# Attention probabilities transposed in 32x32 blocks on VectorE with a transfer through DRAM, and decay matrices with the step size in the exponent

## The chip, the cores and the metric

One Trainium2 chip, one core. The metric is the device time of one execution of the whole kernel in microseconds (us), the median of several timed runs. A profile of one further execution shows every instruction of the engines: PE (TensorE: matmuls, and transposes as matmuls with an identity), PEld (its weight loads), DVE (VectorE), ACT (ScalarE), POOL (GpSimd) and SP, whose queue issues the transfers (DMAs).

## The reference

One layer of a bidirectional encoder over 512 tokens of width 1024, in float32. One projection feeds a state-space branch (Mamba-2 SSD, both directions, 32 heads in 8 groups, chunks of 128 tokens) and a windowed attention branch (16 query heads on 4 key/value heads, width 64, blocks of 128 queries that see 3 blocks of keys, and 2 at either end). Gates merge the branches, an output projection and an MLP follow. The two parts that the change touches, cut to what matters:

```python
# attention, per head and block of 128 queries; keys are 2 or 3 blocks of 128
logits = where(valid, q @ k.T * 64 ** -0.5 + bias, -inf)
m = maximum(logits.max(-1), sink)
p = exp(logits - m)
p = p / (p.sum(-1) + exp(sink - m))
out = p @ v

# SSD within a chunk, per head and direction; cs = cumsum(dt * a)
decay = where(tril, exp(cs[l] - cs[s]), 0)
y_diag[l] = sum over s of (c[l] . b[s]) * decay[l, s] * dt[s] * x[s]
```

## The kernel before

The program is a list of *quanta*. Most are one 128-row tile of a projection: 8 or 16 steps over the contracted dimension, each with three matmuls of 128x512 (`mm3`), since every float32 operand is split into a high and a low part (ACT casts the high part, POOL or DVE subtracts it for the low one). A weight chunk of 512 KB comes by a transfer that SP issues into one of `RAW` = 3 raw buffers and is split into one of `SPL` = 3 pairs of buffers, ahead of the quantum that uses it (`chunk_raw`, `chunk_split`, `prefetch`).

Beside the quanta run *acts*: functions placed at a position between quanta (`at`, `place_head`, `place_ssd`). A position only sets where an act stands in the recorded program. At the end `Planner` reads the whole program with its dependencies, gives every instruction a cost and a due time, and fixes the order of each engine's queue (`chain`). So each engine runs in a fixed order, an instruction that waits holds up those behind it on its own engine, and a change of any operation can move others.

Attention, per head `h`: `attn_bias` loads a bias tile (L849). `attn_scores` makes the scores of 4 query blocks in PSUM, adds the bias and takes the row maximum (DVE, L865), Exp with a sum (ACT, L874), the sums' reciprocal (DVE), and scales each block of probabilities by it (DVE, L880). `attn_flip` transposes the probabilities on PE (L410, 10 blocks of 128x128 a head) into PSUM and copies them out, half on ACT and half on DVE (L891). `attn_values`, for a pair of heads, multiplies the values with them, the two heads side by side in column halves of the array. `HEADS` places the scores at 0, the flip 2 and the values 3.5 quanta behind a head's position; by `JOIN` the values of two pairs are done at one place, four such places in all.

SSD, per group and chunk `c`: `load` brings the rows cs of both directions from DRAM, the same to all partitions (`rf`, `rb`), `similar` the products C.B of two chunks, multiplied by the two triangular masks (L1114), and `prep` makes from them the matrix `m` for 4 heads: POOL subtracts cs from `rb` (L1123), ACT from `rf` (L1125, four pieces of 128), DVE takes the minimum (L1126), ACT Exp (L1127); ACT multiplies the masked products by the step size dt in both directions (L1129 and L1130, eight pieces), DVE adds them and multiplies by the decay (L1131, L1132). `within` uses `m` on PE.

Tiles of 512 columns come from `Slots`, a ring of 73 numbered places that are given out in the order in which they came free.

Of the kernel before, what the change touches and what calls it, by code (L numbers as in the profile page):

```python
# [26 lines left out]
SLOTS, RAW, SPL, PP, AHEAD, SPARE = 73, 3, 3, 3, 4, 6  # L27
# [14 lines left out]
HEADS = dict(scores=0, flip=2, values=3.5)  # L42
# [20 lines left out]
class Slots:  # L63


    def __init__(self, pool, n, tags):
        self.pool, self.free, self.slot, self.n, self.tags = pool, deque(range(n)), {}, 0, tags

    def get(self, name, shape=(128, 512), dtype=F32):
        s = self.free.popleft()  # L70
        self.n += 1
        t = self.pool.tile(list(shape), dtype, tag=f"s{s}", name=f"{name}_{self.n}", bufs=1)
        self.tags[t.tensor.name] = f"s{s}", 1
        self.slot[id(t)] = (s, t)
        return t

    def put(self, *tiles):
        for t in tiles:
            self.free.append(self.slot.pop(id(t))[0])


class Planner:
# [57 lines left out]
    def region(ap):  # L140
# [3 lines left out]
        if step == 0 or ap.tensor.name.startswith(("brow", "csT", "csE", "rrow")):  # L144
# [120 lines left out]
    def transfer(self, n):  # L265
# [3 lines left out]
        rows = {"rrow": 70, "csT": 120, "csE": 100, "in_w_in": 270, "in_w_mlp_in": 270, "in_w_ssd_out": 270, "in_w_attn_out": 270}  # L269
        return size / rows.get(src.tensor.name.rsplit("_", 1)[0].rstrip("01234567") if src.tensor.name.startswith(("cs", "rrow")) else src.tensor.name, 100 if size < 2 ** 17 else 310)  # L270
# [76 lines left out]
class Trunk:  # L347
    def __init__(self, ctx, tc, ins, out, dbg=None):
# [392 lines left out]
    def dt_math(self):  # L741
# [25 lines left out]
        def sums():  # L767
# [7 lines left out]
            nc.vector.tensor_scalar(self.ncs, self.cs, -1.0, None, op0=ALU.mult)  # L775
# [75 lines left out]
    def attn_scores(self, h):  # L851
# [26 lines left out]
        for n in range(4):  # L878
            p, w = P[n]
            nc.vector.tensor_scalar(p[:, :w], p[:, :w], sm[:, n:n + 1], None, op0=ALU.mult)  # L880
        self.P[h] = P

    def attn_flip(self, h):
        self.T[h] = []
        for n, (p, w) in enumerate(self.P.pop(h)):
            pt = self.bank("ps")
            for b in range(w // 128):
                self.tr(pt[:, b * 128:(b + 1) * 128], p[:, b * 128:(b + 1) * 128])
# [2 lines left out]
            (self.nc.vector.tensor_copy if n % 2 else self.nc.scalar.copy)(pT[:, :w], pt[:, :w])  # L891
# [142 lines left out]
    def ssd_steps(self, g):  # L1034
# [71 lines left out]
        def similar(j):  # L1106

            pc, both = self.bank("ps"), get("cb", (128, 2, 2, 128))
# [5 lines left out]
            nc.vector.tensor_tensor(both, products.to_broadcast([128, 2, 2, 128]),  # L1114
# [707 lines left out]
```

## Time and profile before

| what | value |
|---|---|
| timed runs | 1075.16, 1075.75, 1075.84 us; median 1075.75 |
| span of the profiled execution | 1073.7 us; its time beyond the span is not recorded by itself, the timed median is 2.0 us above it |
| TensorE clock granted | 0.999 of full speed |
| DMA | 152.21 MB, mean 142 GB/s |
| attention | DVE reads scores from 51.7 us, PE transposes 58.6 to 328.8, PE values 124.8 to 342.9 |
| last matmul starts | 1067.4 us |

The span is from the first to the last instruction of one execution. "Busy" is time in which an engine runs something; matmuls overlap, so the distance between their starts, not their duration, is what each one takes from PE. "Idle before" is idle time of the engine just before an instruction, with what ended it. A view by windows gives busy us and instructions (x) of each engine in a stretch.

### The profile page before, as it was taken

Reading aid. Unit: us, or ns where it says so; the run is one execution under the profiler, and the core shown is the slowest. Engines: PE = TensorE matmul, PEld = TensorE weight load, DVE = VectorE, ACT = ScalarE, POOL = GpSimd, SP = SyncE. Lnnn points to the kernel's source line nnn. Section 1 sums busy time; section 2 is a strip of 40 time slices with the busy share of each in tenths; the row PEclk is TensorE's granted clock in tenths of the full one; section 3 lists DMA queues with packets and bytes.
Section 4 is the critical chain, followed back from the end, with each engine's and each line's share of the span. In section 5 each row is a group of like instructions: output and inputs, shape, how many; then the busy total and the mean of one; then the engine's idle time right before and its main releaser. Section 6 shows DMA issues by size and latency. Waiting matters only on the chain.

```text
span 1073.7 us, 16828 instructions
## 1 busy us (share of the span) xinstructions
PE 1065.3 (99%) x5560; PEld 898.7 (84%) x5560; DVE 783.9 (73%) x1330; ACT 656.4 (61%) x1413; POOL 809.5 (75%) x1007
## 2 busy tenths in 40 slices
PE   9999999999999999999999999999999999999997
PEld 7888888888888888888888888889888888888886
DVE  6677886798786877778875868769853754764888
ACT  5568776777676867775876522476755444444444
POOL 4546558567648988999998878665999888888853
PEclk9999999999999999999999999999999999999999
DMA  7536425634545655466645399855713512512422
GB/s 209 152 92 165 125 71 143 147 85 133 147 111 146 174 161 158 127 140 177 180 123 133 106 272 323 259 174 150 222 41 93 177 44 88 174 53 75 142 98 79
DMA packets 221560, 152.21 MB, mean 142 GB/s; under 512 B 12541, under 2 KB 195045, under 8 KB 221472
## 3 DMA queue, kind: packets, MB, share of 16 engines
q1 hardware_dynamic: 221324, 151.06, 49.3%
q8 instruction: 44, 0.72, 0.3%
q14 instruction: 44, 0.36, 0.1%
q10 hardware_dynamic: 148, 0.07, 0.0%
HBM read 138.19 MB, written 12.91 MB: 141 GB/s over the span
## 4 chain that ended last, share of the span: by engine, by line
PE 97%; DVE 1%; DMA 0%; ACT 0%; SPq 0%; issue 0%; DVEq 0%; ACTq 0%
PE pp L406 68%; PE ps L406 26%; PE ps L410 4%; DVE x L1731 0%; DMA wr<-in_w_in 0%; DVE C L954 0%; DVE acc L1692 0%; DVE ag L1726 0%; SPq L578 0%; DVE C L961 0%; ACT junk L1712 0%; ACT C L950 0%; DVE junk L627 0%; ACT th L960 0%; SPq L701 0%
## 5 line engine op out<-in xcount | busy, mean ns | idle before, releaser
L406 PE MATMUL pp<-b,wh 128*128 128x512 f32 (+1 forms) x1840 | 564.6, 387 | 0.0
L485 POOL TENSOR_TENSOR wl<-wr,wh 128x256 fp32r<-128x256 f32 (+1 forms) x503 | 416.2, 858 | 137.6 <-ACT wh L481 127.8
L406 PEld LDWEIGHTS pp<-b,wh 128*128 128x128 f32 x1840 | 341.4, 188 | 68.2 <-issue 0.9
L406 PE MATMUL pp<-b,wl 128*128 128x512 f32 (+1 forms) x920 | 355.5, 387 | 0.0
L406 PEld LDWEIGHTS pp<-b,wl 128*128 128x128 f32 x920 | 172.8, 188 | 34.2
L481 ACT CAST wh<-wr 128x1024 fp32r<-128x1024 f32 x131 | 136.3, 1041 | 87.7 <-PE pp L406 65.0
L1646 POOL TENSOR_TENSOR wl<-wd,wh 128x256 fp32r<-128x256 f32 x168 | 147.6, 909 | 39.5 <-ACT wh L1642 25.1
L1642 ACT CAST wh<-wd 128x512 fp32r<-128x512 f32 x108 | 62.9, 619 | 59.9 <-PE pp L406 32.1
L406 PE MATMUL ps<-wh,fh 128*128 128x512 f32 (+1 forms) x196 | 75.5, 385 | 0.5 <-DVE acc L1692 0.5
L406 PE MATMUL ps<-wl,fh 128*128 128x512 f32 (+1 forms) x196 | 75.4, 385 | 0.0
L406 PE MATMUL ps<-wh,fl 128*128 128x512 f32 (+1 forms) x196 | 75.4, 385 | 0.0
L1520 DVE SCALAR_TENSOR_TENSOR pp<-pp,r 128x512 f32<-128x512 f32 (+1 forms) x31 | 17.6, 567 | 67.9 <-ACT r L1517 67.9
L1129 ACT ACTIVATE n<-cb,tables 128x128 f32<-128x128 f32 x128 | 48.9, 393 | 9.4 <-DVE cb L1114 8.9
L1646 POOL TENSOR_TENSOR wl<-wt,wh 128x256 fp32r<-128x256 f32 x56 | 45.8, 849 | 11.0 <-ACT wh L1642 5.7
L1130 ACT ACTIVATE m<-cb,tables 128x128 f32<-128x128 f32 x128 | 49.2, 393 | 5.0 <-DVE cb L1114 3.1
L954 DVE SCALAR_TENSOR_TENSOR u<-pp,cv,u 128x510 f32<-128x510 f32 (+1 forms) x64 | 47.7, 746 | 4.8 <-ACT u L950 3.3
L874 ACT ACTIVATE P<-P,mx 128x384 f32<-128x384 f32 (+1 forms) x64 | 35.2, 552 | 19.1 <-DVE mx L871 18.9
L1181 POOL TENSOR_TENSOR w<-w,E 128x256 f32<-128x256 f32 x48 | 39.5, 838 | 8.7 <-DVE E L1153 7.9
L1123 POOL TENSOR_TENSOR rb<-rb,tables 128x512 f32<-128x512 f32 x32 | 36.4, 1141 | 10.4 <-DMA rb<-csT 10.4
L1125 ACT ACTIVATE rf<-rf,tables 128x128 f32<-128x128 f32 x128 | 42.0, 392 | 2.6 <-DMA rf<-csT 2.5
L406 PEld LDWEIGHTS ps<-wh,fh 128*128 128x128 f32 x196 | 36.8, 188 | 8.1 <-DVE acc L1692 0.7
L406 PEld LDWEIGHTS ps<-wh,fl 128*128 128x128 f32 x196 | 36.8, 188 | 7.4
(304 smaller groups left out, 2064.5 us busy)
## 6 DMA issues: line engine op xcount, KB each, us to landing
wr<-in_w_in SPq DMA_DIRECT2D x74, 512.0 KB, 4.2
wr<-in_w_mlp_in SPq DMA_DIRECT2D x32, 512.0 KB, 4.3
wd<-in_w_mlp_out SPq DMA_DIRECT2D x64, 256.0 KB, 4.0
rb<-csT SPq DMA_DIRECT2D x32, 256.0 KB, 4.9
rf<-csT SPq DMA_DIRECT2D x32, 256.0 KB, 5.1
wr<-in_w_ssd_out SPq DMA_DIRECT2D x14, 512.0 KB, 5.7
wd<-in_w_o SPq DMA_DIRECT2D x28, 256.0 KB, 5.4
E<-csE SPq DMA_DIRECT2D x96, 64.0 KB, 4.8
```

The costliest lines, as they stand in the source:

```text
L406: self.nc.tensor.matmul(out, lhsT, rhs, start=start, stop=stop, skip_group_check=more)
L410: self.nc.tensor.transpose(out, src, self.ident[:n, :n])
L481: self.nc.scalar.copy(hi[:, :m], raw)
L485: engines[e].tensor_tensor(lo[:, c], raw[:, c], hi[:, c].bitcast(F32), op=ALU.subtract)
L954: nc.vector.scalar_tensor_tensor(u[:, a:e], ps[:, a + d:e + d], self.wtap(t, b), u[:, a:e], op0=ALU.mult, op1=ALU.add)
L1123: nc.gpsimd.tensor_tensor(v4(rb), v4(rb), cs[:, 1].unsqueeze(2).to_broadcast([128, 4, 128]), op=ALU.subtract)
L1125: nc.scalar.activation(v4(rf)[:, h], v4(rf)[:, h], AF.Identity, bias=ncs[:, 0, h:h + 1])
L1129: nc.scalar.activation(v4(n)[:, h], cb[:, 0], AF.Copy, scale=dt[:, 0, h:h + 1])
L1130: nc.scalar.activation(v4(m)[:, h], cb[:, 1], AF.Copy, scale=dt[:, 1, h:h + 1])
L1181: nc.gpsimd.tensor_tensor(wc, wc, E[:, d], op=ALU.add)
L1642: nc.scalar.copy(hi, w)
L1646: (nc.vector if e == "v" else nc.gpsimd).tensor_tensor(low[:, q], w[:, q], hi[:, q].bitcast(F32), op=ALU.subtract)
```

## The change

It has two parts, and a third in the memory plan.

1. Attention. ACT instead of DVE scales the probabilities (`NORMED`). In `attn_flip` DVE transposes each 32x32 block of a head's ten 128x128 blocks inside its 32 partitions, into one tile `t` of 128x1280; one transfer writes `t` to DRAM (`pd`), and four transfers, one for each 32 partitions of the result, read it back with the blocks in their places (`pT`). PE's transposes and the copies out of PSUM go. The values matmuls read `pT` with a stride: four runs of 32 elements, 1280 bytes apart. `HEADS` places the flip at 1 and the values at 5.
2. SSD. `nb` = ln(dt) - cs is made once for all heads (one Ln on ACT), and `far` holds 0 inside a mask and -1e30 outside. In `prep` DVE adds `far` to `rf` and POOL to `rb`, ACT takes Exp(r + nb) of each in four pieces, and DVE adds the two and multiplies by the unmasked products C.B, which ACT copies out of PSUM. Two working tiles (`m`, `n`) and one table go.
3. Memory. 58 places of 512 columns instead of 73, and 6 wide ones of 1280 for `t` and `pT`; behind the last values the wide ones are cut into 12 places of 512 for float32 tiles ("carved").

```diff
-SLOTS, RAW, SPL, PP, AHEAD, SPARE = 73, 3, 3, 3, 4, 6
+SLOTS, WIDES, RAW, SPL, PP, AHEAD, SPARE = 58, 6, 3, 3, 3, 4, 6
...
+NORMED = "aaaa"
...
-HEADS = dict(scores=0, flip=2, values=3.5)
+HEADS = dict(scores=0, flip=1, values=5)
...
+    def carve(self, wide):
+        for t in [wide.get("carved") for _ in range(len(wide.free))]:
+            self.free.extend(t[:, i:i + 512] for i in range(0, wide.width - 511, 512))
...
-            nc.vector.tensor_scalar(self.ncs, self.cs, -1.0, None, op0=ALU.mult)
+            nc.vector.tensor_scalar(e, self.dt, 1e-36, None, op0=ALU.max)
+            nc.scalar.activation(e, e, AF.Ln)
+            nc.vector.tensor_tensor(self.nb, e, self.cs, op=ALU.subtract)
...
+            nc.vector.tensor_scalar(self.far, self.UL, -1.0, -NEG, op0=ALU.add, op1=ALU.mult)
...
-            nc.vector.tensor_scalar(p[:, :w], p[:, :w], sm[:, n:n + 1], None, op0=ALU.mult)
+            if NORMED[n] == "a":
+                nc.scalar.activation(p[:, :w], p[:, :w], AF.Copy, scale=sm[:, n:n + 1])
+            else:
+                nc.vector.tensor_scalar(p[:, :w], p[:, :w], sm[:, n:n + 1], None, op0=ALU.mult)
...
     def attn_flip(self, h):
-        self.T[h] = []
-        for n, (p, w) in enumerate(self.P.pop(h)):
-            pt = self.bank("ps")
-            for b in range(w // 128):
-                self.tr(pt[:, b * 128:(b + 1) * 128], p[:, b * 128:(b + 1) * 128])
+        nc = self.nc
+        d = self.dp.tile([128, 1280], F32, name=f"pd{h}")
+        t = self.wides.get("t", (128, 4, 10, 32))
+        x = 0
+        for p, w in self.P.pop(h):
+            nb = w // 128
+            nc.vector.transpose(t[:, :, x:x + nb], p[:, :w].rearrange("p (n b i) -> p b n i", n=nb, i=32))
             self.slots.put(p)
-            pT = self.slots.get("pT", (128, 384))
-            (self.nc.vector.tensor_copy if n % 2 else self.nc.scalar.copy)(pT[:, :w], pt[:, :w])
-            self.T[h].append((pT, w))
+            x += nb
+        nc.sync.dma_start(d, t.rearrange("p b n i -> p (b n i)"))
+        self.wides.put(t)
+        pT = self.T[h] = self.wides.get("pT", (128, 4, 10, 32))
+        for b in range(4):
+            nc.sync.dma_start(pT[b * 32:(b + 1) * 32].rearrange("p a n i -> p a (n i)"),
+                              d[:, b * 320:(b + 1) * 320].rearrange("(a j) x -> j a x", a=4))
...
-                    self.mm(po[u * 64:(u + 1) * 64, n * 128:(n + 1) * 128], v, T[u][n][0][:, b * 128:(b + 1) * 128],
-                            b == 0, b == nb - 1)
+                    self.mm(po[u * 64:(u + 1) * 64, n * 128:(n + 1) * 128], v, T[u][:, :, at + b], b == 0, b == nb - 1)
...
-            nc.vector.tensor_tensor(both, products.to_broadcast([128, 2, 2, 128]),
-                                    self.UL.unsqueeze(1).to_broadcast([128, 2, 2, 128]), op=ALU.mult)
+            nc.scalar.copy(both.rearrange("p u t -> p (u t)"), pc[:, :256])
...
-                nc.gpsimd.tensor_tensor(v4(rb), v4(rb), cs[:, 1].unsqueeze(2).to_broadcast([128, 4, 128]), op=ALU.subtract)
-                for h in range(4):
-                    nc.scalar.activation(v4(rf)[:, h], v4(rf)[:, h], AF.Identity, bias=ncs[:, 0, h:h + 1])
-                nc.vector.tensor_tensor(rf, rf, rb, op=ALU.min)
-                nc.scalar.activation(rf, rf, AF.Exp)
-                for h in range(4):
-                    nc.scalar.activation(v4(n)[:, h], cb[:, 0], AF.Copy, scale=dt[:, 0, h:h + 1])
-                    nc.scalar.activation(v4(m)[:, h], cb[:, 1], AF.Copy, scale=dt[:, 1, h:h + 1])
-                nc.vector.tensor_tensor(m, m, n, op=ALU.add)
-                nc.vector.tensor_tensor(m, m, rf, op=ALU.mult)
+                nb = by_dir(self.nb, c)
+                for d, e in ((0, nc.vector), (1, nc.gpsimd)):
+                    r = (rf, rb)[d]
+                    e.tensor_tensor(v4(r), v4(r), self.far[:, d].unsqueeze(1).to_broadcast([128, 4, 128]), op=ALU.add)
+                    for h in range(4):
+                        nc.scalar.activation(v4(r)[:, h], v4(r)[:, h], AF.Exp, bias=nb[:, d, h:h + 1])
+                nc.vector.tensor_tensor(rf, rf, rb, op=ALU.add)
+                nc.vector.tensor_tensor(v4(rf), v4(rf), cb.unsqueeze(1).to_broadcast([128, 4, 128]), op=ALU.mult)
```

What the planner made of it is seen in the engines' orders. PE first, at the place of the first head's transposes (58.8 us into the span before): `dtw` are the products for the cumulative sums, `P` the probabilities, `b` the normalised input, `wh` and `wl` the two parts of a weight chunk. Before:

```order
L406 MATMUL ps_712<-dtw_430,cst 128x4x32 x2
L406 MATMUL ps_715<-dtw_430,cst 128x256
L410 MATMUL ps_763<-ident,P_638 128x128 x2
L410 MATMUL ps_768<-ident,P_643 128x128 x3
L410 MATMUL ps_774<-ident,P_648 128x128 x3
L410 MATMUL ps_780<-ident,P_653 128x128 x2
L406 MATMUL pp_723<-b_157,wh_576 128x512
L406 MATMUL pp_723<-b_159,wh_576 128x512
```

and now:

```order
L422 MATMUL ps_724<-dtw_430,cst 128x4x32 x2
L422 MATMUL ps_727<-dtw_430,cst 128x256
L422 MATMUL pp_737<-b_157,wh_576 128x512
L422 MATMUL pp_737<-b_159,wh_576 128x512
L422 MATMUL pp_737<-b_157,wl_577 128x512
```

The ten transposes are gone and the next projection's matmuls follow directly; nothing else moved there.

SP's queue next, at the spill of the first attention gate (`gd<-gate`): `wr` are raw weight chunks, `bt` a head's bias, `rf`, `rb` and `E` the rows for SSD. Before:

```order
L928 DMA gd<-gate_1065 128x512
L461 DMA wr_1075<-in_w_in 128x8x128
L461 DMA wr_1149<-in_w_in 128x8x128
L1097 DMA rb_1366<-csT 128x4x128
L1103 DMA E_1369<-csE 64x2x128
L1097 DMA rf_1365<-csT 128x4x128
L1103 DMA E_1369<-csE 64x2x128 x3
L461 DMA wr_1254<-in_w_in 128x8x128
```

and now:

```order
L958 DMA gd<-gate_1060 128x512
L477 DMA wr_1159<-in_w_in 128x8x128
L916 DMA pd_1036<-t_1037 128x1280
L920 DMA pT_878<-pd_871 32x4x320 x4
L868 DMA bt_1328<-brow 128x384
L1133 DMA E_1211<-csE 64x2x128
L1127 DMA rf_1207<-csT 128x4x128
L920 DMA pT_1043<-pd_1036 32x4x320 x4
L477 DMA wr_1239<-in_w_in 128x8x128
```

Between two weight chunks stand the write of one head's blocks and the reads of two heads: a write, four reads of the head before, three other transfers, and then the four reads that wait for that write.

Last the end of DVE's order, from the reciprocal of the last but one normalisation (`frs`) on: `x` are the output pieces, `acc` and `ag` the accumulated and the scaled result. Before:

```order
L1718 RECIPROCAL frs_11488<-frs_11488 128x1
L1722 SCALAR_TENSOR_TENSOR frs_11488<-fsq_11487,frs_11488 128x1
L1731 SCALAR_TENSOR_TENSOR x_1255_11356<-ag_11606,frs_11488,x_1255_11356 128x512
L1731 SCALAR_TENSOR_TENSOR x_1254_11354<-ag_11645,frs_11488,x_1254_11354 128x256
L1692 TENSOR_TENSOR acc_9057<-acc_9057,ps_11627 128x256
L1726 TENSOR_TENSOR ag_11669<-acc_9057,post_mlp_norm_11481 128x256
L1731 SCALAR_TENSOR_TENSOR x_1254_11354<-ag_11645,frs_11488,x_1254_11354 128x256
L1718 RECIPROCAL frs_11488<-frs_11488 128x1
L1731 SCALAR_TENSOR_TENSOR x_1257_11360<-ag_11624,frs_11488,x_1257_11360 128x512
L1731 SCALAR_TENSOR_TENSOR x_1256_11358<-ag_11669,frs_11488,x_1256_11358 128x256 x2
```

and now:

```order
L1742 RECIPROCAL frs_10946<-frs_10946 128x1
L1746 SCALAR_TENSOR_TENSOR frs_10946<-fsq_10945,frs_10946 128x1
L1755 SCALAR_TENSOR_TENSOR x_1132_10826<-ag_10968,frs_10946,x_1132_10826 128x512
L1755 SCALAR_TENSOR_TENSOR x_1127_10816<-ag_11061,frs_10946,x_1127_10816 128x512
L1716 TENSOR_TENSOR acc_8571<-acc_8571,ps_11082 128x256
L1750 TENSOR_TENSOR ag_11124<-acc_8571,carved_3956 128x256
L1755 SCALAR_TENSOR_TENSOR x_1126_10814<-ag_11100,frs_10946,x_1126_10814 128x256
L1742 RECIPROCAL frs_10946<-frs_10946 128x1
L1755 SCALAR_TENSOR_TENSOR x_1129_10820<-ag_11079,frs_10946,x_1129_10820 128x512
L1755 SCALAR_TENSOR_TENSOR x_1126_10814<-ag_11100,frs_10946,x_1126_10814 128x256
L1755 SCALAR_TENSOR_TENSOR x_1128_10818<-ag_11124,frs_10946,x_1128_10818 128x256 x2
```

A 512-wide piece now stands where a 256-wide one stood ahead of the last `acc`, and one more 256-wide piece stands behind the last reciprocal.

More of the change, by code (lines that the diff above doesn't have):

```diff
@@ L63, with __init__, get @@
 class Slots:
-    def __init__(self, pool, n, tags):
+    def __init__(self, pool, n, tags, width=512, prefix="s"):
         self.pool, self.free, self.slot, self.n, self.tags = pool, deque(range(n)), {}, 0, tags
-    def get(self, name, shape=(128, 512), dtype=F32):
-        s = self.free.popleft()
-        self.n += 1
-        t = self.pool.tile(list(shape), dtype, tag=f"s{s}", name=f"{name}_{self.n}", bufs=1)
-        self.tags[t.tensor.name] = f"s{s}", 1
+        self.width, self.prefix = width, prefix
+    def get(self, name, shape=None, dtype=F32):
+        shape = shape or (128, self.width)
+        s = next(s for s in self.free if dtype == F32 or isinstance(s, int))
+        self.free = deque(x for x in self.free if x is not s)
+        self.n += 1
+        if isinstance(s, int):
+            tag = f"{self.prefix}{s}"
+            t = self.pool.tile(list(shape), dtype, tag=tag, name=f"{name}_{self.n}", bufs=1)
+            self.tags[t.tensor.name] = tag, 1
+        else:
+            t = s[:, :math.prod(shape[1:])]
+            if len(shape) > 2:
+                names = "abcd"[:len(shape) - 1]
+                t = t.rearrange(f"p ({' '.join(names)}) -> p {' '.join(names)}", **dict(zip(names, shape[1:])))
         self.slot[id(t)] = (s, t)
@@ L143, in region @@
         step = dims[0][0]
-        if step == 0 or ap.tensor.name.startswith(("brow", "csT", "csE", "rrow")):
+        if step == 0 or ap.tensor.name.startswith(("brow", "csT", "csE", "rrow", "pd")):
             lo = ap.offset
@@ L268, in transfer @@
         size = 4 * math.prod(d[1] for d in dst.ap)
-        rows = {"rrow": 70, "csT": 120, "csE": 100, "in_w_in": 270, "in_w_mlp_in": 270, "in_w_ssd_out": 270, "in_w_attn_out": 270}
-        return size / rows.get(src.tensor.name.rsplit("_", 1)[0].rstrip("01234567") if src.tensor.name.startswith(("cs", "rrow")) else src.tensor.name, 100 if size < 2 ** 17 else 310)
+        rows = {"rrow": 70, "csT": 120, "csE": 100, "pd": 200, "in_w_in": 270, "in_w_mlp_in": 270, "in_w_ssd_out": 270, "in_w_attn_out": 270}
+        return size / rows.get(src.tensor.name.rsplit("_", 1)[0].rstrip("0123456789") if src.tensor.name.startswith(("cs", "rrow", "pd")) else src.tensor.name, 100 if size < 2 ** 17 else 310)
     def plan(self, wait=0.3):
@@ L744, in dt_math @@
         bias = self.dt_bias
-        self.tables = [get("tables", (128, 2, 4, 64)) for _ in range(3)]
-        self.ncs = self.tables[2][:, 0]
-        self.dt, self.cs, self.dec, self.coef = (self.tables[i // 2][:, i % 2] for i in range(4))
+        self.tables = [get("tables", (128, 2, 4, 64)) for _ in range(2)]
+        self.dec, self.coef, self.nb, far = (self.tables[i // 2][:, i % 2] for i in range(4))
+        self.far = far.rearrange("p c h -> p (c h)").rearrange("p (d t) -> p d t", d=2)
+        dtc = get("dtc", (128, 2, 4, 64))
+        self.dt, self.cs = (dtc[:, i] for i in range(2))
         v = self.dtv
@@ L898, in attn_values @@
         po = self.bank("ps")
+        at = 0
         for n in range(4):
-            nb = T[0][n][1] // 128
+            nb = 3 if n in (1, 2) else 2
             for b in range(nb):
```

20 lines of the change are left out of this document (9 added, 11 removed).

## The prediction

> **What bounds the kernel now.** I read the page first (busy shares, then the chain that ended last), then the busy time by stage, then TensorE's groups and its instructions in order of time, and only then the other engines' groups, the transfers and the waits.
>
> ```profile
> span 1073.7 us, 16828 instructions
> PE 1065.3 (99%) x5560; PEld 898.7 (84%) x5560; DVE 783.9 (73%) x1330; ACT 656.4 (61%) x1413; POOL 809.5 (75%) x1007
> ...
> PE 97%; DVE 1%; DMA 0%; ACT 0%; SPq 0%; issue 0%; DVEq 0%; ACTq 0%
> ```
>
> The chain is TensorE for 97% of the span; nothing else holds more than 1%. A busy TensorE need not be a full one, so the stages come next.
>
> ```profile
> 60.00:340.00 280.00, 280.00 (x1699) 240.04 (x1700) 223.68 (x475) 203.55 (x493) 176.97 (x232) 1.00 0.46 122
> 340.00:600.00 260.00, 259.81 (x1422) 219.20 (x1417) 194.78 (x274) 183.48 (x416) 236.38 (x285) 1.00 0.59 154
> 600.00:1074.00 474.00, 467.18 (x2155) 390.43 (x2153) 327.84 (x503) 235.23 (x435) 368.25 (x448) 1.00 0.46 143
> ```
>
> Columns: length, then busy us of PE, PEld, DVE, ACT, POOL, the granted clock, the DMA share and GB/s. Attention lies in the first stage. There PE has no idle time at all, DVE has 56 us (280 - 223.7), ACT 76, POOL 103, and the clock is full. So a PE instruction that goes from that stage takes its time with it, unless another engine is made late by more than its idle time.
>
> **The transposes on TensorE.** The change takes away all 160 of the attention's. The first row is from the groups by line and shape (busy us, mean ns, idle before), the others from the instructions in order of time (start us, us, how many).
>
> ```profile
> L410 PE MATMUL ps<-ident,P 128*128 128x128 f32 x160 | 21.0, 274 | 0.0
> ...
> 57.95 1.04 PE L406 MATMUL ps<-dtw,cst 128*128 128x128 f32 x6
> 58.84 1.25 PE L410 MATMUL ps<-ident,P 128*128 128x128 f32 x10
> 59.85 0.71 PE L406 MATMUL pp<-b,wh 128*128 128x512 f32 x2
> 60.40 0.39 PE L406 MATMUL pp<-b,wl 128*128 128x512 f32 x1
> 60.63 0.62 PE L406 MATMUL pp<-b,wh 128*128 128x512 f32 x2
> 61.08 0.39 PE L406 MATMUL pp<-b,wl 128*128 128x512 f32 x1
> ```
>
> The mean of one, 274 ns, is pipeline time; what the next work waits is the distance of starts. Ten transposes start at 58.84 and the next matmul at 59.85: 1.01 us. The two matmuls behind them take 0.55 us (59.85 to 60.40) where the same pair takes 0.45 a little later (60.63 to 61.08): 0.10 us more for the change of kind. So 1.11 us for ten, 0.111 each, and 160 x 0.111 = **17.8 us**. The busy time, 21.0, is an upper bound (it counts the overlap with what follows), 160 x 0.101 = 16.2 a lower one; I take 17.8.
>
> The Trainium skill, "TensorE: Matmul & The Clock Gate", Part 4 (PE-mode transpose), gives about 275 ns for one 128x128 transpose in a kernel's context. The trace has the same 274 ns as a duration, but starts 0.11 us apart; by the page's figure the sum would be 44 us, by the distances it is 17.8.
>
> The values matmuls stay, 160 in the program, but now read their moving operand as four runs of 32 elements, 1280 bytes apart. The nearest row is `ps<-dtw,cst` above: two of its three products read four runs of 32 at a stride. It shows six records, two of them twice as wide, in 0.89 us (57.95 to 58.84), 0.111 for each 128 columns, against twelve contiguous ones in 1.34 us, 0.112 each:
>
> ```profile
> 303.12 1.50 PE L406 MATMUL ps<-C,pv 128*128 128x128 f32 x12
> 304.46 0.61 PE L406 MATMUL ps<-C,B 128*128 128x128 f32 x4
> ```
>
> I take nothing for the stride.
>
> **The work on DVE and ACT.** DVE loses the normalisation and half the copies out of PSUM, and gets 64 block transposes.
>
> ```profile
> L880 DVE TENSOR_SCALAR P<-P,sm 128x384 f32<-128x384 f32 x32 | 17.3, 573 | 0.0
> L880 DVE TENSOR_SCALAR P<-P,sm 128x256 f32<-128x256 f32 x32 | 14.2, 442 | 0.6
> L891 DVE COPY pT<-ps 128x384 f32<-128x384 f32 x16 | 8.8, 548 | 3.5 <-PE ps L410 3.4
> L891 DVE COPY pT<-ps 128x256 f32<-128x256 f32 x16 | 6.7, 417 | 3.9 <-PE ps L410 3.9
> L754 DVE RECIPROCAL dtw<-dtw 128x256 f32<-128x256 f32 x1 | 1.8, 1752 | 0.0
> ```
>
> Removed: 17.3 + 14.2 + 8.8 + 6.7 = 47.0 us. The trace has no block transpose. Its ends: a copy of the same width (0.55 and 0.42 us, so 32 x 0.548 + 32 x 0.417 = 30.9 us), and the slowest DVE row for its width, the reciprocal (1.75 us for 256, 2.63 for 384: 140 us). A transpose moves data as the copy does and computes nothing, so I take the copy: DVE is lighter by 16 us, and that buys nothing, since DVE does not bound.
>
> ```profile
> L982 ACT ACTIVATE w<-u,dcol 128x256 f32<-128x256 f32 x32 | 14.9, 503 | 2.6 <-DMA gd<-gate 1.3 <-DVE u L961 1.2
> L1125 ACT ACTIVATE rf<-rf,tables 128x128 f32<-128x128 f32 x128 | 42.0, 392 | 2.6 <-DMA rf<-csT 2.5
> L1127 ACT ACTIVATE rf<-rf 128x512 f32<-128x512 f32 x32 | 19.7, 625 | 6.5 <-DVE rf L1126 6.5
> L1129 ACT ACTIVATE n<-cb,tables 128x128 f32<-128x128 f32 x128 | 48.9, 393 | 9.4 <-DVE cb L1114 8.9
> L621 ACT ACT_TABLE_LOAD x1 | 1.3, 1283 | 1.9 <-issue 1.9
> ```
>
> ACT gets the 64 normalisations. At 256 wide one costs L982's 0.50; at 384 between that and L1127's 0.63 for 512, say 0.56: 34 us, in a stage with 76 us idle, and it loses its own 32 copies. In the decay matrices it loses twelve 128-wide pieces and one Exp for each of 32 chunks (12 x 0.392 + 0.625 = 5.3 us) and gets eight pieces (3.1), 70 us less over eight groups, and sixteen copies more. The logarithm brings two more table loads, 2.6 us near 57 us into the span, hidden behind weights that were loaded chunks ahead (below). POOL keeps one 512-wide addition a chunk. DVE keeps three operations of 512 a chunk (add, add, multiply for min, add, multiply), and the product with the masks goes. All this shortens chains beside a PE that waits for none of them: **0 us**. If the cover were gone, a late `m` would hold the within-chunk matmuls, but its chain only gets shorter.
>
> **The transfers.** For each head one write of 640 KB to DRAM and four reads of 160 KB back: 16 x 1.31 MB = 21 MB in some 280 us, 75 GB/s on top of the stage's 122, which by that ratio lifts its DMA share from 0.46 to some 0.74. The rows are from the DMA issues (KB each, us to landing), the chain in order of time (start, length) and the waits of SP's queue (us in all, times, longest).
>
> ```profile
> gd<-gate SPq DMA_DIRECT2D x16, 256.0 KB, 2.4
> x1d<-x SPq DMA_DIRECT2D x8, 256.0 KB, 7.4
> rb<-csT SPq DMA_DIRECT2D x32, 256.0 KB, 4.9
> ...
> 52.62 5.49 PE pp L406 x24
> ...
> SPq L461 <- POOL wl L485: 279.7, 102, 9.8
> ```
>
> From issue to landing a write of 256 KB takes 2.4 to 7.4 us, a spread read 4.9. Transposes (1.9) + write + read: 1.9 + 7.4 + 4.9 = 14.2 us; were the write to grow with its size, 1.9 + 18.5 + 4.9 = 25.3. The values stand four quanta behind the flip, and a quantum holds at least the 24 matmuls of one tile, 5.49 us: 22 us. So I take **0**, and keep up to 3.3 us at each of four places where values are joined, 13 us, for the range.
>
> On SP's queue a read waits for the write's landing, with the weight loads, the rows of csT and csE and the gate spills queued behind it. Loads are issued when POOL has freed a raw buffer (SP waits 279.7 us for that), and with three raw and three split buffers run about five quanta, 27 us, ahead of PE. A block of a few us on SP is inside that.
>
> One wait is new on DVE: the first addition of a chunk now waits for the row rf from DRAM, where ACT waited (2.5 us in all, L1125's row). Behind it on DVE stand the convolutions and the score reductions, which free PSUM banks for PE. With 56 us idle I take 0, and at most the 10 us that POOL waits for the other row:
>
> ```profile
> POOL rb L1123 <- DMA rb<-csT: 10.4, 6, 4.2
> ```
>
> **The end.** The order of DVE's last operations moves, and there PE no longer hides them.
>
> ```profile
> 1066.60 1.14 DVE L1731 SCALAR_TENSOR_TENSOR x<-ag,frs,x 128x512 f32<-128x512 f32 x2
> 1067.73 0.42 DVE L1692 TENSOR_TENSOR acc<-acc,ps 128x256 f32<-128x256 f32 x1
> 1068.18 0.43 DVE L1726 TENSOR_TENSOR ag<-acc,post_mlp_norm 128x256 f32<-128x256 f32 x1
> ...
> 1069.25 1.54 DVE L1731 SCALAR_TENSOR_TENSOR x<-ag,frs,x 128x512 f32<-128x512 f32 x3
> ```
>
> Before, a 512- and a 256-wide piece fill the 1.1 us up to the last accumulation, and three pieces follow the last reciprocal (1.54 us: 512, 256, 256). Now two 512-wide ones stand ahead (some 0.35 us longer) and four pieces follow (one more of 256, 0.4): **+0.75 us**, between 0 and 1.
>
> **The sum.** Span 1073.7 - 17.8 + 0.75 = 1056.7 us. The timed median, 1075.75, is 2.0 us above this span, and I carry that over: **1058.7 us**.
>
> **The rivals.**
> 1. *Small new waits (0.15).* Blocks of some heads land late or DVE stands before rf. For it: the 25.3 against 22 us above, and a queue that serves in order. Against it: 14.2 by the rows as they are. Price 2 to 15 us: 1061 to 1074, half of it below 1065.
> 2. *DVE becomes the bound: slower than before (0.03).* If one block transpose cost as much as the reciprocal, DVE's load in 60 to 340 us would grow by 140 - 47 = 93 us against 56 idle: 37 us in which PE waits for banks and blocks, and 1058.7 + 37 = 1096. It decides from (56 + 47) / 64 = 1.6 us a transpose; from (56 + 47 + 17) / 64 = 1.9 us the kernel is slower than before.
> 3. *The move through DRAM is slow by its pattern (0.02).* Each read scatters four source rows into every partition. If reads landed in 19 times the 4.9 us of rb<-csT, 93 us, each of four joined places would wait 1.9 + 7.4 + 93 - 22 = 80 us: 1379. Against it: both sides run 1280 bytes contiguously, no element is strided. The Trainium skill, "VectorE: DVE Perf Modes", The three transpose paths, warns that a plain copy that transposes by strides is 19 times slower; no run here shows that.
> 4. *A transpose is worth its full 274 ns (0.03)*: 44 us, 1032. The distances of starts speak against it.
> 5. *The PE time is given back elsewhere, no gain (0.03)*: the weights' split (POOL) would have to limit the shortened stage; but POOL has 103 us idle there, and where it is full (236 of 260 us, the next stage) no transposes go. 1075.75.
>
> **How the numbers follow.** Forecast 0.74, with the bounds of its own terms 1054.8 (21.0 us, nothing at the end) to 1060.5 (16.2 us, 1 at the end). The range takes in that and the lower half of rival 1: 1054.8 to 1064.5, leaving out 0.11 for rivals 2 to 5 and some 0.07 of rival 1. Faster by over 0.2% (2.2 us, about what a measurement of this kernel can tell from no change): 0.74 + 0.14 + 0.03 = 0.91; within: 0.01 + 0.03 = 0.04; slower: 0.03 + 0.02 = 0.05.
>
> **What would show it.** Right: no `ident,P` group; PE busy down by 17 to 21 us with idle time as before; the stage up to the last values shorter by some 18 us and the others equal; block transposes at 0.4 to 0.6 us. Wrong: PE idle with DMA `pT<-pd` as releaser (rivals 1, 3), DVE near full with transposes over 1.6 us (2), `pT,V` matmuls further than 0.112 us apart, or SP long in waits for `pd`.

## The result and the profile after

| | before | after | predicted |
|---|---|---|---|
| time, median (us) | 1075.80 | 1060.75 | 1058.7 (1054.8 to 1064.5) |
| ratio, 95% interval | | 0.9853 [0.9841, 0.9866] | 0.984 |
| profiled execution: span (us) | 1073.7 | 1059.1 | 1056.7 |
| start of TensorE's last matmul (us) | 1067.41 | 1052.09 | 1049.6 (1067.4 - 17.8) |

The kernel is 15.05 us faster (1075.80 - 1060.75); the forecast was 2 us too low. The page of the changed kernel first: the span, the busy shares and the chain that ended last.

```profile
span 1059.1 us, 16498 instructions
PE 1048.9 (99%) x5400; PEld 881.7 (83%) x5400; DVE 769.2 (73%) x1284; ACT 628.2 (59%) x1304; POOL 820.0 (77%) x1007
...
PE 98%; DVE 1%; DMA 0%; issue 0%; SPq 0%; ACT 0%; DVEq 0%
```

TensorE has 160 instructions fewer (5560 to 5400) and 16.4 us less busy time (the prediction named 17 to 21 as its sign), and it still holds the chain. The next view is busy time by stage; columns as before: length, PE, PEld, DVE, ACT, POOL, clock, DMA share, GB/s. The bounds lie 10 to 15 us earlier than those shown of before.

```profile
60.00:330.00 270.00, 270.00 (x1584) 228.88 (x1584) 213.67 (x444) 203.58 (x473) 186.77 (x240) 1.00 0.77 206
330.00:590.00 260.00, 258.78 (x1403) 218.54 (x1402) 194.13 (x261) 155.74 (x331) 242.43 (x282) 1.00 0.56 152
```

The attention stage has no idle time on TensorE, although its DMA share went from 0.46 to 0.77. The middle stage has 1.2 us of idle time where it had 0.2 before. Then the new operations: the groups by line and shape (busy us, mean ns, idle before), and the DMA issues (KB, median us to landing).

```profile
L900 ACT ACTIVATE P<-P,sm 128x384 f32<-128x384 f32 x32 | 18.8, 609 | 4.2 <-DVE mx L890 2.8 <-DVE sm L896 1.5
L913 DVE STREAM_TRANSPOSE t<-P 128x384 f32<-128x384 f32 x32 | 17.4, 561 | 4.0 <-ACT P L900 4.0
L900 ACT ACTIVATE P<-P,sm 128x256 f32<-128x256 f32 x32 | 15.3, 501 | 0.3 <-DVE sm L896 0.3
L913 DVE STREAM_TRANSPOSE t<-P 128x256 f32<-128x256 f32 x32 | 13.0, 420 | 3.0 <-ACT P L900 2.9
...
pd<-t SPq DMA_DIRECT2D x16, 640.0 KB, 5.2
pT<-pd SPq DMA_DIRECT2D x64, 160.0 KB, 5.0
```

A block transpose costs what a copy of that width cost (0.548 and 0.417 us before; 0.561 and 0.420 now). The write of 640 KB lands in 5.2 us (writes of 256 KB took 2.4 and 7.4 us before), and no read of the wide tile took more than 5.9 us: rival 3 is out.

**Where the missing 2 us are.** In order of time, the chain of waits between 420 and 435 us (start, length):

```profile
428.92 1.21 issue
430.12 0.68 PE ps L422 x4
```

Four transposes of B have ended, and the four products of C and B start 1.2 us late. What they need is C, which comes from its weight matmuls by a first step on ScalarE (L950, now L980), four on VectorE, a tanh on ScalarE and a last product on VectorE (L961, now L991). These are lines of the engines' orders of time at this place, before:

```profile
436.86 0.78 ACT L950 ACTIVATE C<-pp,cv 128x512 f32<-128x512 f32 x1 [0.49 <-PE pp L406]
439.01 2.84 PE L406 MATMUL ps<-m,x 128*64 128x128 f32 x48
441.53 0.83 DVE L961 SCALAR_TENSOR_TENSOR C<-th,C 128x512 f32<-128x512 f32 x1 [0.16 <-ACT th L960]
442.42 0.71 PE L406 MATMUL ps<-C,B 128*128 128x128 f32 x4
```

and after ("carved" are buffers cut from the freed wide tiles; here they hold C, B and, in the first line, a decay matrix):

```profile
422.99 1.28 ACT L1154 ACTIVATE carved<-carved,tables 128x128 f32<-128x128 f32 x4 [0.85 <-DVE carved L1152]
424.18 0.76 ACT L980 ACTIVATE carved<-pp,cv 128x512 f32<-128x512 f32 x1
428.83 1.19 DVE L991 SCALAR_TENSOR_TENSOR carved<-carved,carved 128x512 f32<-128x512 f32 x1 [0.76 <-ACT carved L990]
430.12 0.68 PE L422 MATMUL ps<-carved,carved 128*128 128x128 f32 x4 [1.22 <-issue]
```

The profile names no releaser for this wait ("issue"), but the times leave little doubt: VectorE's last product ends at 430.02 us, and TensorE starts at 430.12 (before: 442.36 and 442.42). Before, ScalarE waited for C's last weight matmul and began 0.04 us behind its end, at 436.86. After, that matmul ends at 423.02 (it starts at 422.63), but ScalarE begins at 424.18, 1.16 us late: it first waits 0.85 us for VectorE's new addition (L1152) and then makes four Exp pieces of a decay matrix, which stand ahead of C in its order. What TensorE does in the meantime has not become shorter. Before it is ten weight matmuls, 48 within-chunk matmuls and the transposes of B, 5.8 us in all (436.65 to 442.42); after it is a whole tile of 24 weight matmuls and the transposes, 6.0 us (422.86 to 428.90). Without the late start the wait would be some 0.1 us, an estimate from these lines (1.22 - 1.16); experiment 10 has such a start.

### The profile page after: what moved, and what is told of

Read it like the earlier page. It is cut to its first block, busy times and chain, and to the rows that moved or that the text cites. A ratio compares the mean times of both kernels' runs of the same rounds, so it can differ in the third digit from the quotient of the medians.

```text
span 1059.1 us, 16498 instructions
## 1 busy us (share of the span) xinstructions
PE 1048.9 (99%) x5400; PEld 881.7 (83%) x5400; DVE 769.2 (73%) x1284; ACT 628.2 (59%) x1304; POOL 820.0 (77%) x1007
## 4 chain that ended last, share of the span: by engine, by line
PE 98%; DVE 1%; DMA 0%; issue 0%; SPq 0%; ACT 0%; DVEq 0%
PE pp L422 69%; PE ps L422 27%; PE ps L426 2%; DVE x L1755 0%; DMA wr<-in_w_in 0%; DVE acc L1716 0%; DVE ag L1750 0%; SPq L594 0%; ACT carved L1736 0%; DVE junk L643 0%; DVE frs L1742 0%; ACT frs L1741 0%; SPq L717 0%; SPq L718 0%; DVEq L1842 0%
## 5 line engine op out<-in xcount | busy, mean ns | idle before, releaser
L1670 POOL TENSOR_TENSOR wl<-carved,wh 128x256 fp32r<-128x256 f32 x110 | 98.0, 917 | 20.1 <-ACT wh L1666 12.4
L1670 POOL TENSOR_TENSOR wl<-wd,wh 128x256 fp32r<-128x256 f32 x78 | 67.9, 897 | 17.9 <-ACT wh L1666 15.2
L1666 ACT CAST wh<-carved 128x512 fp32r<-128x512 f32 x69 | 40.7, 618 | 44.8 <-PE pp L422 20.8
L1666 ACT CAST wh<-wd 128x512 fp32r<-128x512 f32 x49 | 29.0, 618 | 26.0 <-PE pp L422 11.3
L984 DVE SCALAR_TENSOR_TENSOR u<-pp,cv,u 128x510 f32<-128x510 f32 (+1 forms) x52 | 38.8, 747 | 6.8 <-ACT u L980 5.7
L422 PEld LDWEIGHTS ps<-wl,fh 128*128 128x128 f32 x196 | 36.8, 188 | 7.4
L1544 DVE SCALAR_TENSOR_TENSOR pp<-pp,r 128x512 f32<-128x512 f32 (+1 forms) x18 | 10.7, 592 | 41.2 <-ACT r L1541 41.1
L1670 POOL TENSOR_TENSOR wl<-wt,wh 128x256 fp32r<-128x256 f32 x36 | 32.0, 917 | 10.4 <-issue 4.8
L1154 ACT ACTIVATE rb<-rb,tables 128x128 f32<-128x128 f32 x100 | 32.6, 393 | 11.9 <-POOL rb L1152 11.9
L1205 POOL TENSOR_TENSOR w<-w,E 128x256 f32<-128x256 f32 x38 | 34.0, 905 | 4.5 <-DVE E L1177 3.6
```

The lines of the kernel that those rows point to most:

```text
L422: self.nc.tensor.matmul(out, lhsT, rhs, start=start, stop=stop, skip_group_check=more)
L984: nc.vector.scalar_tensor_tensor(u[:, a:e], ps[:, a + d:e + d], self.wtap(t, b), u[:, a:e], op0=ALU.mult, op1=ALU.add)
L1154: nc.scalar.activation(v4(r)[:, h], v4(r)[:, h], AF.Exp, bias=nb[:, d, h:h + 1])
L1205: nc.gpsimd.tensor_tensor(wc, wc, E[:, d], op=ALU.add)
L1544: nc.vector.scalar_tensor_tensor(dst[:, tok], ps[:, tok], 0.0, r[:, tok], op0=ALU.max, op1=ALU.mult)
L1666: nc.scalar.copy(hi, w)
```

## The experiments

All times are medians; each ratio is to the kernel before, timed beside it on the same chip, with its 95% interval. **Theory A** is the prediction's: the gain is the start distance of the 160 transposes, and the rest lies beside TensorE. Attention's part alone, with the old decay matrices, was not run; experiment 2 takes its transposes back instead.

**1. The decay matrices alone** (attention as before):

```
 self.mm(pc[...], B, C)            # kept
-tensor_tensor(both, products, UL, mult);  ... Identity, min, Exp, Copy*dt, Copy*dt, add, mult
+scalar.copy(both, pc)
+tensor_tensor(r, r, far, add); activation(r, Exp, bias=nb) for each head and direction; add; mult
```

> The change's decay matrices alone (step size in the exponent); attention as before, with its 160 transposes on TensorE. Theory A (the gain is the 160 transposes at 0.111 us each, and the lighter decay matrices lie beside a TensorE that does not wait): no gain, 1074.5 to 1077 us, TensorE busy about 1065, ScalarE about 70 us lighter. Rival B (the lighter ScalarE and VectorE give part of the gain): 1065 to 1073 us.

Measured 1075.59 us, ratio 0.9999 [0.9990, 1.0009]. TensorE's busy time stays (1064.8 us, 1065.3 before). The decay matrices' own groups on ScalarE fall from 159.8 to 84.1 us, with 6.0 of new copies, and its busy time falls from 656.4 to 611.8 (neighbours that overlap count once there): it buys nothing. Rival B falls.

**2. The transposes back on TensorE**, all else as changed:

```
-nc.vector.transpose(t[...], p[...]); dma t -> pd; 4 x dma pd -> pT
+self.tr(pt[...], p[...]) for each block; copy pt -> pT (half VectorE, half ScalarE)
```

> The changed kernel, with all 160 blocks transposed by TensorE again and copied out of PSUM into the same wide tiles; no block transposes on VectorE and no transfers through DRAM. All else as changed: normalising on ScalarE, the flip's and the values' places, strided reading, decay matrices. Theory A: the whole gain goes, 1075 to 1079 us (1060.75 + 160 x 0.111 = 1078.5, less whatever waits the changed kernel has and this one has not). Rival B (part of the gain is elsewhere in the change): 1066 to 1073. Rival C (the transfers take back part of the gain, so that TensorE's own share is larger than 17.8): above 1080.

Measured 1077.62 us, ratio 1.0011 [1.0000, 1.0022]: the whole gain is gone. TensorE's groups here, and the values matmuls before (last line):

```profile
L426 PE MATMUL ps<-ident,P 128*128 128x128 f32 x160 | 20.4, 274 | 0.0
L422 PE MATMUL ps<-pT,V 128*64 128x128 f32 x320 | 18.4, 274 | 0.0
L406 PE MATMUL ps<-pT,V 128*64 128x128 f32 x320 | 18.4, 274 | 0.0
```

The values matmuls read the same strided tile as in the changed kernel and take 18.4 us in all and 274 ns each, as they did before: no cost of the stride shows. The transposes are worth 1077.62 - 1060.75 = 16.9 us by the medians, 0.105 each; in the profiled executions the last matmul starts 16.3 us later than in the changed kernel (1068.39 against 1052.09), 0.102 each.

**3. Half of the heads on TensorE** (`if h % 4 < 2:` VectorE and DRAM, else TensorE):

> As the previous, with half of the heads by TensorE (80 transposes) and half by VectorE and DRAM. Theory A, each transpose worth its distance of starts: half-way, 1060.75 + 80 x 0.111 = 1069.6, between 1067.5 and 1070.5. If the gain were one step (a wait that is there or not there), it would lie near one end: under 1063 or over 1074.

Measured 1069.88 us, ratio 0.9934 [0.9921, 0.9947]. With 0, 80 and 160 transposes the kernel takes 1060.75, 1069.88 and 1077.62 us: steps of 9.1 and 7.7, a straight line within 1 us, and nothing like one step. Theory A.

**4. One more hop in the transfers' chain:**

```
-nc.sync.dma_start(d, t)
+nc.sync.dma_start(d0, t)
+nc.sync.dma_start(d, d0)
```

(Here and in 5 and 12 the planner's table of transfer rates names the new DRAM tile as well.)

> The changed kernel with one more transfer, DRAM to DRAM, of each head's 640 KB between the write and the four reads: some 5 us more in every head's chain and 21 MB more traffic. Theory A (the chain of some 12 us lies inside 22 us of four tiles' matmuls): 1060.5 to 1062. Rival 1 of the prediction (the chain is near its limit, blocks land late): each of four joined places late by 3 us or more, 1065 to 1080, with TensorE idle on the wide tile at L422.

Measured 1100.2 us, ratio 1.0222 [1.0208, 1.0236]: a miss, 39 us where at most 1 was expected, and not by rival 1's mechanism either: no wait of TensorE is ended by a landing of the wide tile. Its largest wait from 60 to 330 us (us in all, times, longest):

```profile
PE pp L422 <- ACT wh L497: 8.8, 4, 4.0
```

It waits for split weights (`wh`), and it is idle for 12 of the 100 us from 200 on:

```profile
200.00:260.00 60.00, 54.17 (x329) 44.14 (x328) 40.99 (x84) 35.61 (x80) 37.75 (x49) 0.97 0.70 196
260.00:300.00 40.00, 33.78 (x190) 26.73 (x190) 20.76 (x47) 21.81 (x53) 13.67 (x20) 0.91 0.83 210
```

Behind 57 us TensorE is idle for 23.5 us where the changed kernel has 1.7; part of the rest is the clock, which is below 1.00 in both stretches. SP's queue in order of time shows one link:

```profile
243.18 0.38 SPq L477 DMA_DIRECT2D wr<-in_w_in  x1
...
254.47 2.51 SPq L917 DMA_DIRECT2D pe<-t  x2
257.03 2.44 SPq L922 DMA_DIRECT2D pT<-pd  x4
259.58 0.40 SPq L477 DMA_DIRECT2D wr<-in_w_in  x1
```

For 16 us no weights are loaded: writes of heads stand ahead of them and wait until VectorE has made their blocks (254.47). In all SP waits 42.7 us for blocks, up to 14.3 at a time, where the changed kernel has 16.8 and 3.2. Pairing each load of `w_in` with the first matmul that uses it, in order, gives the lead of the loads over TensorE. For the weights that are used between 100 and 390 us it is never under 25.4 us before and 24.7 after, and 10.9 with the hop.

That is not the whole way to the longest stop, 3.95 us at 276.94. Its weights were issued at 259.58, 17.4 us ahead, and landed at about 265.3; their cast starts at 275.86, because ScalarE has other work ahead of it in its order, above all the probabilities of two heads:

```profile
263.80:276.00 12.20, 9.19 (x44) 7.34 (x42) 9.37 (x29) 12.09 (x37) 1.24 (x3) 1.00 0.98 306
```

ScalarE is busy for 12.09 of these 12.20 us. So the hop moved the orders of several engines against each other; SP's blocked queue is one of the causes, and its share is open.

**5. The hop's bytes without its wait** (the second write goes to a place that nobody reads):

```
 nc.sync.dma_start(d, t)
+nc.sync.dma_start(d0, t)
```

> The extra hop cost some 39 us; this run has its bytes without its wait. The changed kernel with a second write of each head's 640 KB to another place in DRAM that nobody reads: the same 10.5 MB more as the hop, the same number of issues on SP, but nothing waits for the extra write to land. Theory D (the hop's cost is SP's queue: each wait for a landing holds up the weight loads queued behind it): 1060 to 1064 us. Rival E (the hop's cost is bandwidth: the stage's DMA share of 0.77 has no room for 10.5 MB): 1075 to 1100.

Measured 1077.96 us, ratio 1.0015 [1.0002, 1.0028]. By the number that is rival E's range, but not by the place of the loss. In the stage itself:

```profile
60.00:325.00 265.00, 265.00 (x1531) 224.30 (x1530) 207.22 (x436) 195.97 (x464) 170.78 (x219) 1.00 0.80 224
```

At 224 GB/s TensorE has no idle time, so the stage bears the bytes. The loss lies behind it: at 330 us, where the last values meet a DMA share of 1.07 (330 to 335 us), and at 500 us, where attention has no transfers left:

```profile
505.70 0.80 PE L422 MATMUL ps<-xl,bt 128*128 128x512 f32 x1 [1.77 <-DVE xl L1089]
509.09 0.80 PE L422 MATMUL ps<-xl,bt 128*128 128x512 f32 x1 [2.17 <-DVE xl L1089]
```

The planner writes one order for all engines from modelled times, so 16 more transfers also move work that has nothing to do with them. The run does not separate D and E. Against E: the 12 idle us of experiment 4 between 200 and 300 us came at 201 GB/s on average, and here the same stretch has 230 GB/s and no idle time. Against D as it was put: here, too, SP waits 34.3 us for VectorE's blocks, up to 12.4 at a time, and the lead of the weights falls to 10.1 us at 267 us, yet TensorE does not stop there. A blocked queue and a short lead are thus not enough for a stop.

**6. Every block transpose twice** (`for _ in range(2): nc.vector.transpose(...)`):

> The changed kernel with every block transpose done twice by VectorE (64 more, 30.4 us, in a stage where VectorE is idle for 56 of 270 us). Theory A (VectorE has room beside TensorE): 1060.5 to 1063. Rival 2 of the prediction, taken to this size (VectorE near its bound, each added us shows): 1075 to 1091, TensorE idle with VectorE as releaser.

Measured 1062.86 us, ratio 0.9875 [0.9858, 0.9891]; the profiled execution took 1060.38. VectorE in 60 to 330 us rises from 213.7 to

```profile
60.00:330.00 270.00, 270.00 (x1579) 228.14 (x1578) 237.35 (x507) 202.15 (x468) 183.98 (x237) 1.00 0.77 205
```

237.4 us, and TensorE stays at 270.00 of 270. Theory A: VectorE has room. (The three other executions lie 2.2 to 2.9 us above the profiled one; what they lost, no trace shows.)

**7. The same move for x and B** in the state space part (a block transpose, a write of 256 KB and four reads for each of 24 tiles; 96 transposes off TensorE):

```
-self.tr(pt[...], st["u"][i][:, tok]) ...; self.tr(pt[...], st["B"][...])
+self.move(u, ...) behind x's silu; self.move(st["B"], ...) behind B's; copies and splits read the landed tile
```

> The same move done to 96 more transposes of TensorE, those of x (64) and B (32) in the state space part: block transposes on VectorE, one 256 KB write and four 64 KB reads for each of 24 tiles. Theory A with a start distance of 0.102 to 0.111 us each: 9.8 to 10.7 us less than the changed kernel, 1050 to 1051 us. Rival D (24 more waits on SP's queue hold up weight loads, as in the run with the hop): above 1061.

Measured 1087.14 us, ratio 1.0100 [1.0085, 1.0115]: slower than both kernels. SP's waits:

```profile
SPq L1000 <- DVE t L998: 35.8, 8, 10.7
```

Who waited for the landed tile, from its own view:

```profile
DVE bt L440: 13.2, 4
PEld ps L422: 4.0, 6
```

The writes hold SP's queue up to 10.7 us until VectorE has its blocks, and B's split, whose input is a landing, keeps VectorE standing for 13.2 us. The number is in rival D's range, and SP's waits are its sign; but TensorE's longest waits, 4.5 and 3.1 us, are for convolutions on VectorE, and how much of the loss the weights have was not separated.

**8. The deferred within-chunk matmuls one quantum later** (`DEFER_BY = 9` to `10`), a test of the 1.2 us at 429 us:

> The changed kernel with the deferred within-chunk matmuls of two groups placed one quantum later (10 in place of 9 after the group), so that nine more weight matmuls (2 us) lie between the last matmul of C and the C x B products at 429 us. Theory F (the new idle of 1.2 us there is C's convolution, uncovered because the masks, ready earlier, let TensorE take the within-chunk matmuls a tile sooner): 1.0 to 1.4 us less, 1059.2 to 1060.0, no idle over 0.5 us before the C x B products. Rival G (ScalarE or VectorE is late there for another reason): the idle stays, 1060.4 to 1061.

Measured 1064.36 us, ratio 0.9881 [0.9865, 0.9897]: 3.6 us slower than the changed kernel, where 1.0 to 1.4 us less were expected. At the place itself the wait is gone. TensorE in order of time:

```profile
426.53 0.60 PE L426 MATMUL ps<-ident,carved 128*128 128x128 f32 x4
427.06 1.53 PE L422 MATMUL ps<-rf,x 128*64 128x128 f32 x24
428.95 0.71 PE L422 MATMUL ps<-carved,carved 128*128 128x128 f32 x4
```

Thirty-two within-chunk matmuls (24 shown, 8 more behind them) stand ahead of the products of C and B again. This does not decide for theory F, though: the order of ScalarE moved too, and here C's first step starts as soon as C's weight matmuls end (at 420.83 us). Experiment 10 decides it. The gain is lost again at 597 us, where the other deferred group is now late: the sum for the norm waits 1.8 us for VectorE.

```profile
597.69 0.50 PE L422 MATMUL ps<-sl,ones_r 128*128 128x512 f32 x1 [1.82 <-DVE sl L440]
```

**9. Every block transpose four times**, 1.9 us for each tile, the point that the prediction gave for "slower than before":

> The changed kernel with every block transpose done four times by VectorE: 4 x 0.475 = 1.9 us for each tile, the point from which rival 2 of the prediction has the kernel slower than before. VectorE's work in 60 to 330 us becomes 213.7 + 3 x 30.4 = 305 us in a stage of 270. Rival 2's arithmetic: at least 35 us more than the changed kernel, 1090 to 1105, the loss inside the attention stage. If VectorE's other work can move out of the stage: 1062 to 1080.

Measured 1090.19 us, ratio 1.0142 [1.0126, 1.0158]: 29 us more than the changed kernel, where rival 2's arithmetic asked for at least 35. The transposes take 111.4 us where 122 were reckoned, 81 more than before this edit; with 56 idle, the same arithmetic gives 25.

```profile
60.00:330.00 270.00, 254.01 (x1446) 210.99 (x1446) 259.84 (x582) 187.29 (x439) 170.99 (x216) 0.99 0.71 187
```

VectorE is at 260 of 270 us, TensorE loses 16 us in this window alone. The mechanism of rival 2 is real; the transpose is four times too cheap for it.

**10. Less cover for the transfers** (`HEADS values=5` to `3.5`):

> The changed kernel with the values 2.5 quanta after the flip in place of 4 (some 8 us less cover for the transfers' chain). In the changed kernel the last read of a wide tile is issued at least 11.5 us before TensorE uses it (median 25) and lands in 5. Theory A (the chain is hidden with some 6 us to spare at its tightest place): within 2 us of the changed kernel where the heads spread as evenly, or a few waits of 2 to 3 us on the wide tile, 1060 to 1068. Rival 1 (the prediction's cover of four quanta was just enough): every head late, 16 x 2 us or more, above 1080.

Measured 1060.71 us, ratio 0.9860 [0.9848, 0.9873]: no difference. Reads land in 5.4 us (median), and no wait of TensorE is ended by one. The span is 1058.6, and the wait at 429 us is absent. The engines' orders of time at that place:

```profile
422.64 1.28 ACT L1154 ACTIVATE carved<-carved,tables 128x128 f32<-128x128 f32 x4 [3.52 <-DVE carved L1152]
424.35 0.78 ACT L980 ACTIVATE carved<-pp,cv 128x512 f32<-128x512 f32 x1 [0.43 <-PE pp L422]
429.03 0.72 DVE L991 SCALAR_TENSOR_TENSOR carved<-carved,carved 128x512 f32<-128x512 f32 x1 [0.43 <-ACT carved L990]
430.03 0.61 PE L422 MATMUL ps<-carved,carved 128*128 128x128 f32 x4
```

This decides what the new wait was. As in the changed kernel, a tile of 24 weight matmuls and the transposes of B are all that stands behind C's tile, and no within-chunk matmul does. But here the four Exp pieces are done before C's weight matmuls end, ScalarE waits 0.43 us for TensorE instead of the other way round, and TensorE has no idle time. (VectorE's last product is 0.47 us shorter here, too; the late start alone is 1.16 of the 1.22 us.)

**11. x alone, in groups 3 to 7**, with half a quantum more cover:

> The move by VectorE and DRAM done to x as well, in groups 3 to 7 alone (40 transposes of TensorE), with half a quantum more for the transfers, and not to B. Theory A (each transpose gone is worth 0.102 to 0.111 us where the transfers find cover): 4.1 to 4.4 us less than the changed kernel, 1056 to 1057. Rival D (writes wait on SP's queue for VectorE and hold up the weights, as with x and B): 1061 to 1075.

Measured 1070.54 us, ratio 0.9950 [0.9938, 0.9962]: 10 us more than the changed kernel. TensorE stands for 3.9 us near 491 us, for `xh`, the split of the weighed x. The chain that led there waits 5.8 us for a row of csT (from 480.8) and then passes through POOL's weighing, additions and a weight split from 488.2 to 494.5. In that stretch POOL is busy 48.2 of 50 us (47.1 in the changed kernel, where TensorE does not stop):

```profile
450.00:500.00 50.00, 46.09 (x219) 38.61 (x218) 40.65 (x56) 27.92 (x61) 48.22 (x56) 0.97 0.65 176
```

So a later x falls on an engine without room to catch up; whether SP's order or POOL weighs more here was not separated.

**12. The hop again, with 4 us more counted for its landings in the planner:**

```
 free[e], end = end, queue + self.TAIL
+if the transfer reads or writes pd or pe: end += 4000
```

> The kernel with the extra hop again, same transfers, same bytes; alone the planner that writes SP's order now counts 4 us more for the landing of every transfer of the probabilities, so that what waits for them stands later in SP's queue. Theory D (the hop's 39 us are SP's order: blocking waits ahead of weight loads): at least half comes back, 1062 to 1080 us. Rival E (the chain itself is too long for the cover, or the traffic too much): 1095 to 1105, TensorE idle on the wide tiles.

Measured 1089.0 us, ratio 1.0107 [1.0085, 1.0128]: 11 of the 39 us come back from the planner's order alone, less than the half that was expected. TensorE again waits for weights, not for the wide tile:

```profile
PE pp L424 <- ACT wh L499: 10.3, 2, 6.7
```

Rival E's sign, waits on the wide tile, comes to 0.4 us. SP still waits 38 us for VectorE's blocks, which no landing estimate changes. What share of the rest bytes have is open. No kernel here beats the changed one beyond its spread.

## Why the prediction was right

- **The bound.** TensorE, chain 97%: right. 160 instructions less showed as time (2, 3); 45 us less of ScalarE's busy time did not (1).
- **The price of a transpose.** 0.111 us was predicted, between 0.101 and 0.131. The last matmul starts 15.33 us earlier although TensorE is idle for 1.0 us more behind 57 us (1.7 against 0.7), so its own work is 16.3 us shorter, 0.102 each; the undo (2) gives the same 16.3. So the term of 17.8 us was mis-sized by some 1.5 us. The distance of starts, 0.101, was right; the 0.10 us for the change of kind was counted for each ten transposes. But in TensorE's order of time, the stream of weight matmuls was interrupted by fp32 work 47 times before and is interrupted 43 times after: most transposes stood beside other fp32 work that pays the change anyway. 160 x 0.101 = 16.2 us is nearly all of it; what the four changes are worth is too small to be read here (experiment 10 is interrupted 47 times, and its own work is 15.6 us shorter). An estimate by the 275 ns that the Trainium skill gives for bf16 ("TensorE: Matmul & The Clock Gate", Part 4) would have been 44 us; the trace's row of 274 ns is a duration of matmuls that overlap.
- **The stride**: nothing, as predicted (2).
- **VectorE and ScalarE.** Block transposes 30.4 us against 30.9; normalisations 34.1 against 34. VectorE fell by 14.7 us in all (16 predicted).
- **The transfers, 0 predicted.** Right: write 5.2, read 5.0, with the transposes 12.1 us where 14.2 were reckoned, and the view of the wide tile has 0.2 us of waiting for it in it. Experiment 10 takes 8 us of cover away at no cost. But "a block of a few us on SP is inside" the lead of the weights was right with less room than it sounded: one more transfer in each head's chain costs 39 us (4).
- **Nothing new to wait for, 0 predicted.** Wrong by 1.0 us, and not at `rf`, where I looked: the new wait is for C at 429 us. The step that failed is "All this shortens chains beside a PE that waits for none of them". The total of the work fell, but its pieces stand in ScalarE's order among others, and TensorE does wait for one chain that passes there: C's, on which it had waited 0.2 us already before. Four Exp pieces, late behind VectorE's new addition, held up C's first step by 1.16 us. Where they are done in time (10), the wait is gone.
- **The end.** +0.64 us (from the end of the last matmul to the end of the span 6.05, now 6.69), 0.75 predicted, for the reason given: four pieces behind the last reciprocal.

```profile
1051.27 1.41 DVE L1755 SCALAR_TENSOR_TENSOR x<-ag,frs,x 128x512 f32<-128x512 f32 x2
1052.59 0.41 DVE L1716 TENSOR_TENSOR acc<-acc,ps 128x256 f32<-128x256 f32 x1
...
1054.10 1.94 DVE L1755 SCALAR_TENSOR_TENSOR x<-ag,frs,x 128x512 f32<-128x512 f32 x4
```

- **The sum.** 1073.7 - 16.3 + 1.0 + 0.64 = 1059.0, against 1059.1 measured. This closes almost by construction, since the 16.3 is read from the same starts; the check from outside is experiment 2. Two terms missed the same way, 1.5 and 1.0 us, and the 2.0 us between span and timed median came out 0.3 smaller, so the miss of 2.4 us in the span shows as 2.05 in the time. 1060.75 lies just outside what the forecast's own terms allowed (1054.8 to 1060.5) and inside the part of the range that was added for small new waits. One of the signs was badly chosen: the stage up to the last values is only 10.4 us shorter (342.9 to 332.5), because the values themselves stand one and a half quanta later.

## What to carry to other kernels

Price an instruction that leaves a bound engine by the distance of starts, and do not count a change of kind for each group that goes while other work of the same kind stands beside it. Idle time of an engine over a stage does not say that its order is harmless: look at what stands ahead of the work on which the bound engine waits next. Work can be moved to transfers, but measure what they do to the engines' orders: here one more transfer in each head's chain cost 39 us, while the same bytes without that wait left the stage without idle time and cost 17 us behind it. The same move did not pay for x and B; in the stage behind attention POOL is busy for 242 of 260 us, and whether that or SP's order weighs more is open.

## What the runs showed of the hardware

A short stop of TensorE cost more than itself. In experiment 8 one idle of 1.82 us (and 0.23 shortly before) was followed by matmuls 0.43 us apart in place of 0.23. Busy time by stretches of 2.5 us (the last three numbers: granted clock, DMA share, GB/s):

```profile
595.00:597.50 2.50, 0.87 (x3) 0.39 (x3) 2.50 (x2) 1.21 (x3) 2.08 (x1) 1.00 0.53 160
597.50:600.00 2.50, 2.31 (x7) 1.85 (x8) 2.50 (x6) 1.52 (x2) 0.18 (x1) 0.73 0.01 3
600.00:602.50 2.50, 2.50 (x8) 1.97 (x7) 2.50 (x3) 0.00 (x0) 2.50 (x1) 0.59 0.34 106
```

In these stretches the granted clock fell to 0.73 and 0.59; from 598.63 to 602.04 us, 3.41 us, it was 0.50, and from 602.5 us 1.00. The idle of 1.21 us at 429 us in the changed kernel left it at 1.00 in each stretch of 2 us from 426 to 436. The Trainium skill ("TensorE: Matmul & The Clock Gate", Part 1) gives an idle window of about 3.4 us before the clock halves; here less than that was enough. So the price of a wait is not linear in these two places: 1.2 us cost 1.2, while 1.8 us cost some 3.4 (the wait, and eight matmuls from 598.8 us on at 0.2 more each).
